# Order and engines of the post-norm chains, the gate rows and the final norm in a two-block transformer kernel

## The chip, the cores and the metric

The kernel runs on one core of a Trainium2 chip. The metric is the device time of one execution in microseconds (us). All times below were taken on the chip; the profile is that of one execution.

## The reference, cut to what matters

Two transformer blocks are computed for one sequence of 256 tokens of width 2048, all in f32. In the first block the vector c gives six rows of modulation; g_a and g_f are the gates.

```python
mod = c_act @ ada_w + ada_b
sh_a, sc_a, g_a, sh_f, sc_f, g_f = jnp.split(mod, 6, axis=-1)
h = modulate(rms_norm(x, attn_pre_norm), sh_a, sc_a)
y = hybrid_mixer(h, ...)                     # latent and differential attention, ends in @ w_o
x = x + g_a[:, None, :] * rms_norm(y, attn_post_norm)
h = modulate(rms_norm(x, ffn_pre_norm), sh_f, sc_f)
y = conv_geglu_ffn(h, w_up, conv_w, conv_b, w_down)
x = x + g_f[:, None, :] * rms_norm(y, ffn_post_norm)
# second block
h = rmsnorm(x, norm_g); proj = h @ w_in_2    # sparse and windowed attention
x = x + concat([y_a, y_b]) @ w_out_2
out = rmsnorm(x, final_g)
```

## The kernel before, in words

**Weights.** All weights come as one stream of pieces of 512 KB, [128 x 1024] f32, which SP's queue loads into twelve buffers (`raw`, line 270). Most pieces are split into a high part, rounded to the one-pass type fp32r (`hi`, a cast on ScalarE, line 292), and the rest (`lo`, a subtraction on VectorE, line 293). A product is then three one-pass matmuls: x_hi with hi, x_hi with lo, x_lo with hi. Only the modulation takes raw f32 weights: on TensorE in products of 32 rows (line 472), or on VectorE (lines 514 to 516).

**Order.** The program is a list of units of weights. Between units, small pieces of other work written as generators (softmax, gates, statistics) are advanced by a turn each; a `yield` leaves the rest to a later turn. Each engine has one queue, executed in order; a scheduler sets what stands in it from these turns and the dependences.

**Places that the change touches.** `job_y` multiplies the two token halves t = 0, 1 (128 rows each) by four groups of 512 columns, n (g in the code) = 0 to 3, one k tile after the other; it computes w_o, w_down and w_out. At its last k tile the sums go to `y_stats`, which adds the earlier part (line 1208), multiplies by the gate row (line 1213) and takes three sums of squares and products (lines 1212, 1215, 1216). In `p_ffn` the first YK of the 44 k tiles of w_down are done amid the work on w_up and the others at the end.

When all groups are in, `post` reduces the sums over the groups and computes two reciprocal roots for the two token halves: ry, that of y's post-norm, and r1, that of the new x's pre-norm, which is formed from the sums without the new x itself. Each root is a scaling (line 606), a square root on ScalarE (line 607) and four steps on VectorE (lines 608 to 611). Then `make_h` goes through eight pairs of k tiles: `x_new` updates x (line 1247) and scales it by r1 (line 1249), `x_turn` transposes it on TensorE (line 700) and writes the modulated high and low parts for the products (lines 1272 to 1274, or 1266 and 1267 in block 2). The next stage's first product is line 331. There are two such junctions: out of w_o into the FFN, and out of w_down into block 2.

The gates are made ahead of that. `gate_start` loads four rows `gw` and a bias `brow`. For the attention, `ada_rows` adds `brow` to the modulation's sum in PSUM (line 563) and spreads each of four rows over all partitions by a product with a constant (line 567). For the FFN, `ada_fold` does the same for one group at a time (lines 577 and 580). At the end `fin` computes the last root for both halves and scales and stores eight tiles (lines 1497 to 1500).

Of the kernel before, what the change touches and what calls it, by code (L numbers as in the profile page):

```python
# [13 lines left out]
F32 = mybir.dt.float32  # L14
F32R = mybir.dt.float32r
# [120 lines left out]
class Body:  # L136
# [295 lines left out]
    def job_y(self, mat, groups, kts, x, evac):  # L432
        out = []
        kts = list(kts)
        box = {}
        for n, kt in enumerate(kts):
            for g in groups:
                def fn(wt, o, n=n, kt=kt, g=g):
                    mm = self.nc.tensor.matmul
                    hi, lo = wt  # L440
                    f, l = n == 0, n == len(kts) - 1
                    if f and o == 0:
                        box[g] = [self.ps() for _ in range(2)]
                    c = slice(o * 128, o * 128 + hi.shape[-1])
                    xk = x(kt)
                    for t in range(2):
# [111 lines left out]

    def ada_rows(self, ps):
        nc = self.nc  # L560
        self.gate_start(0)
        sb = self.w()
        nc.vector.tensor_tensor(out=sb, in0=self.brow, in1=ps, op=ALU.add)
        yield
        for n in range(4):
            ps2 = self.ps()
            nc.tensor.matmul(ps2, self.cst("jsel", n, n + 1).to_broadcast([P, P]), sb, start=True, stop=True)
            yield
            nc.vector.tensor_tensor(out=self.gw[n], in0=self.gw[n], in1=ps2, op=ALU.mult)
            self.gdone[n] = True  # L570

    def ada_fold(self, acc, n):
        nc = self.nc
        a = slice(32 * n, 32 * n + 1)
        if n == 0:
            self.gate_start(1)
        nc.vector.tensor_tensor(out=acc[a], in0=acc[a], in1=self.brow[a], op=ALU.add)
        yield
        ps = self.ps()
        nc.tensor.matmul(ps, self.cst("ones"), acc, start=True, stop=True)  # L580
        yield
        nc.vector.tensor_tensor(out=self.gw[n], in0=self.gw[n], in1=ps, op=ALU.mult)
        self.gdone[n] = True


    def split(self, dst, src):
# [140 lines left out]
    def setup(self):  # L727
# [21 lines left out]
        nc.scalar.dma_start(self.ct, self.io["cst"])  # L749
        nc.scalar.dma_start(self.vt, self.io["vecs"])  # L750
        self.mod = cp.tile([P, 96], F32, tag="mod", name="mod")
        self.dtab = cp.tile([P, 3, 8, 4], BF16, tag="dtab", name="dtab")
        cb = self.cb = cp.tile([P, 5, P], BF16, tag="cb", name="cb")
        self.identb, self.mcau, self.mband = cb[:, 0], cb[:, 1:3], cb[:, 3:5]
# [81 lines left out]
    def small(self):  # L836
        nc = self.nc
        V, S = nc.vector, nc.scalar
        l4 = self.vec("lam")
        pr, ls, le = self.s(64), self.s(2), self.s(2)  # L840
        for j in range(2):
# [376 lines left out]

    def rowsum(self, a):
        o = self.s(2)  # L1220
        self.nc.vector.tensor_reduce(out=o, in_=a.rearrange("p (t n) -> p t n", t=2), axis=AX.X, op=ALU.add)
        return o

    def post(self):
        V = self.nc.vector
        sy, sxz, szz = self.rowsum(self.sy), self.rowsum(self.sxz), self.rowsum(self.szz)
        ry = self.ry = self.rsqrt_fast(sy, 2, 1.0 / D)
        t = self.s(2)
        V.tensor_tensor(out=t, in0=szz, in1=ry, op=ALU.mult)
        V.tensor_tensor(out=t, in0=sxz, in1=t, op=ALU.add)  # L1230
        V.tensor_tensor(out=t, in0=t, in1=ry, op=ALU.mult)
        V.tensor_tensor(out=self.sxx, in0=self.sxx, in1=t, op=ALU.add)
        self.r1 = self.rsqrt_fast(self.sxx, 2, 1.0 / D)
        self.gw = self.brow = None
        self.hs = {}
        self.xr = {}

    def x_new(self, i):
        V = self.nc.vector
        n, o = i // 2, (i % 2) * T  # L1240
        xr = self.xr[i] = self.w()
        with self.tc.issue_after(self.rs.ins):
            for t in range(2):
                x, z = self.xn[n, t], self.accy[n, t]
                if i < 2 or o == 0:
# [3 lines left out]
                V.tensor_scalar(out=xr[:, t * T:t * T + T], in0=x[:, o:o + T], scalar1=self.r1[:, t:t + 1], scalar2=None,  # L1249
                                op0=ALU.mult)  # L1250

    def x_turn(self, i, al, sh):
        nc = self.nc
        V, S = nc.vector, nc.scalar
        xr = self.xr.pop(i)
        ps = self.ps()
        for j in range(2):
            for t in range(2):
                self.transpose(ps[:, j * T + t * 128:j * T + t * 128 + 128], xr[:, t * T + j * 128:t * T + j * 128 + 128])
        for j in range(2):  # L1260
            k = 2 * i + j
            src = ps[:, j * T:j * T + T]
            a = al[:, k:k + 1]
            h = self.hs[k] = self.g(F32R)
            if sh is None:
                S.activation(h[:, :T], src, AF.Identity, bias=0.0, scale=a)
                V.scalar_tensor_tensor(out=h[:, T:], in0=src, scalar=a, in1=h[:, :T].bitcast(F32),
                                       op0=ALU.mult, op1=ALU.subtract)
            else:
                b = sh[:, k:k + 1]  # L1270
                f = xr[:, j * T:j * T + T]
                S.activation(h[:, :T], src, AF.Identity, bias=b, scale=a)  # L1272
                S.activation(f, src, AF.Identity, bias=b, scale=a)
                V.tensor_sub(h[:, T:], f, h[:, :T].bitcast(F32))

    def make_h(self, kt, al, sh):
        if kt == 0:
# [69 lines left out]
    def p_block2(self):  # L1347
# [123 lines left out]
        def mid2():  # L1471
            self.fg = [self.g() for _ in range(4)]
            for n in range(4):
                nc.sync.dma_start(self.fg[n], self.io["rows"][8 + n])
            self.sy = self.s(8)
            self.load_sqrt()

        def ev2(n, t, ps):
            x = self.xn[n, t]
            c = slice(4 * t + n, 4 * t + n + 1)  # L1480
            V.tensor_add(x, x, ps)
            sq = self.w()
            S.activation(sq, x, AF.Square, accum_out=self.sy[:, c])
            o = self.xn[n, t] = self.g()
# [5 lines left out]

        def fin():
            self.drain()
            r = self.rsqrt_fast(self.rowsum(self.sy), 2, 1.0 / D)
            for i, (n, t) in enumerate(sorted(self.xn)):
                a = self.xn[n, t]
                if i % 3 == 2:
                    S.activation(a, a, AF.Identity, scale=r[:, t:t + 1], bias=0.0)
                else:
                    V.tensor_scalar(out=a, in0=a, scalar1=r[:, t:t + 1], scalar2=None, op0=ALU.mult)
                nc.sync.dma_start(self.io["out"][4 * t + n], a)  # L1500
        return prog + self.call(fin)

    def compress(self, src, mat, pcol):
# [326 lines left out]
```

## Time and profile before

| | |
|---|---|
| Times of three runs, us | 1708.7, 1703.77, 1709.03 (median 1708.7) |
| Profiled execution, us | 1710.42 |
| its span, first to last instruction, us | 1708.5 |
| mean granted TensorE clock | 0.983 |
| PE busy | 1652.9 us, 97% |
| VectorE (DVE) busy | 1222.6 us, 72% |
| ScalarE (ACT) busy | 929.8 us, 54% |
| GpSimd (POOL) busy | 9.1 us, 1% |
| read from memory | 378.83 MB, 223 GB/s over the span |

Times inside the span count from its start. Shares of busy time are means over stages. PE is TensorE, PEld its weight load, SP the engine that issues most loads and stores. In a row of the timeline, the number in brackets is the engine's idle time ahead of the instruction, with what ended it. A granted clock of 1.00 is TensorE's full speed of 2.4 GHz, 0.50 the lower one of 1.2 GHz. In names of matmuls, `ps<-hi,g` is a product of tiles hi and g summed into PSUM.

### The profile page before, as it was taken

How to read it: one execution, taken by the hardware profiler on the slowest of the kernel's cores; microseconds unless marked ns; L12 is line 12 of the kernel's file. 1: busy time of each engine (PE TensorE's matmuls, PEld its weight loads, DVE VectorE, ACT ScalarE, POOL GpSimd, SP SyncE). 2: the span in 40 equal slices, each digit the busy share in tenths (PEclk: the TensorE clock that was granted, in tenths of full speed). 3: DMA queues.
4: the chain of work that ended last, by engine and by line, in shares of the span. 5: the costliest groups of instructions: out<-in, count | busy, mean ns of one | idle time of the engine just before them, and what ended most of it. 6: DMA issues, size and time to landing. Idle time of an engine off the chain costs nothing.

```text
span 1708.5 us, 27826 instructions
## 1 busy us (share of the span) xinstructions
PE 1652.9 (97%) x9968; PEld 1363.4 (80%) x9968; DVE 1222.6 (72%) x2499; ACT 929.8 (54%) x1949; POOL 9.1 (1%) x25
## 2 busy tenths in 40 slices
PE   6999999899979999999999999999979999999997
PEld 3778877667559888888888888888869888888885
DVE  6766678676776987888556777776676767777765
ACT  3444448545446766666444566665544445555643
POOL 0000000000000000000000000000000000000000
PEclk8999999999989999999999999999989999999998
DMA  9878975787965667666666665555645773344451
GB/s 381 319 280 301 335 271 186 265 348 305 387 249 169 218 222 252 223 226 217 237 221 242 220 203 186 189 187 191 195 143 176 249 255 131 124 140 140 144 185 50
DMA packets 108138, 382.74 MB, mean 224 GB/s; under 512 B 12128, under 2 KB 12384, under 8 KB 108000
## 3 DMA queue, kind: packets, MB, share of 16 engines
q1 hardware_dynamic: 107136, 379.28, 63.7%
q8 instruction: 78, 1.28, 0.3%
q10 hardware_dynamic: 864, 1.69, 0.3%
q14 instruction: 60, 0.49, 0.1%
HBM read 378.83 MB, written 2.10 MB: 223 GB/s over the span
## 4 chain that ended last, share of the span: by engine, by line
PE 93%; DVE 3%; DMA 2%; ACT 1%; issue 0%; ACTq 0%; SPq 0%; DVEq 0%
PE ps L339 24%; PE ps L340 12%; PE ps L449 8%; PE ps L450 8%; PE ps L451 8%; PE ps L331 6%; PE ps L332 5%; PE ps L333 5%; PE ps L472 4%; PE ps L700 2%; PE ps L423 2%; PE ps L424 1%; PE ps L425 1%; DVE lo L293 1%; PE ps L1690 1%; PE ps L1006 1%
## 5 line engine op out<-in xcount | busy, mean ns | idle before, releaser
L292 ACT CAST hi<-raw 128x512 fp32r<-128x512 f32 x989 | 610.0, 622 | 588.9 <-PE ps L339 194.0
L293 DVE TENSOR_TENSOR lo<-raw,hi 128x512 fp32r<-128x512 f32 x989 | 672.7, 689 | 308.9 <-ACT hi L292 303.7
L339 PE MATMUL ps<-g,hi 128*128 128x512 f32 x1744 | 621.9, 401 | 0.0
L340 PE MATMUL ps<-g,lo 128*128 128x256 f32 x1744 | 489.8, 281 | 0.0
L339 PEld LDWEIGHTS ps<-g,hi 128*128 128x128 f32 x1744 | 327.6, 188 | 82.8 <-issue 2.4
L340 PEld LDWEIGHTS ps<-g,lo 128*128 128x128 f32 x1744 | 329.6, 189 | 0.8 <-issue 0.7
L449 PE MATMUL ps<-hi,g 128*128 128x512 f32 x608 | 240.9, 398 | 1.5 <-ACT hi L292 1.5
L450 PE MATMUL ps<-lo,g 128*128 128x512 f32 x608 | 237.1, 390 | 0.6 <-DVE lo L293 0.6
L451 PE MATMUL ps<-hi,g 128*128 128x512 f32 x608 | 237.1, 390 | 0.0
L331 PE MATMUL ps<-g,hi 128*128 128x256 f32 x752 | 220.9, 296 | 1.2 <-ACT g L1272 0.7
L332 PE MATMUL ps<-g,hi 128*128 128x256 f32 x752 | 214.0, 285 | 0.0
L333 PE MATMUL ps<-g,lo 128*128 128x256 f32 x752 | 213.7, 285 | 0.0
L331 PEld LDWEIGHTS ps<-g,hi 128*128 128x128 f32 x752 | 144.9, 194 | 24.5 <-ACT hi L292 12.4
L332 PEld LDWEIGHTS ps<-g,hi 128*128 128x128 f32 x752 | 145.5, 194 | 2.4 <-issue 1.4
L333 PEld LDWEIGHTS ps<-g,lo 128*128 128x128 f32 x752 | 145.3, 193 | 0.8 <-issue 0.8
L449 PEld LDWEIGHTS ps<-hi,g 128*128 128x128 f32 x608 | 113.7, 188 | 39.5 <-issue 7.8
L450 PEld LDWEIGHTS ps<-lo,g 128*128 128x128 f32 x608 | 114.2, 188 | 25.9 <-DVE lo L293 2.7
L451 PEld LDWEIGHTS ps<-hi,g 128*128 128x128 f32 x608 | 114.1, 188 | 24.1
L516 DVE SCALAR_TENSOR_TENSOR w<-raw,csil,w 128x512 f32<-128x512 f32 x105 | 78.7, 749 | 21.1 <-DMA raw<-wstream 20.2
L472 PE MATMUL ps<-raw,cz 128*32 128x512 f32 (+1 forms) x608 | 83.0, 582 | 0.0
L938 DVE TENSOR_TENSOR g<-g,ps 128x512 f32<-128x512 f32 (+1 forms) x48 | 31.8, 664 | 44.0 <-PE ps L333 43.9
L700 PE MATMUL ps<-ct,w 128*128 128x128 f32 x248 | 37.8, 279 | 18.8 <-DVE w L1249 18.8
(273 smaller groups left out, 1510.5 us busy)
## 6 DMA issues: line engine op xcount, KB each, us to landing
raw<-wstream SPq DMA_DIRECT2D x704, 512.0 KB, 4.3
g<-rows SPq DMA_DIRECT2D x12, 256.0 KB, 4.5
g<-xt SPq DMA_DIRECT2D x8, 256.0 KB, 5.5
g<-xn SPq DMA_DIRECT2D x8, 256.0 KB, 5.4
out<-g SPq DMA_DIRECT2D x8, 256.0 KB, 2.8
g<-brow SPq DMA_DIRECT2D x2, 256.0 KB, 5.8
g<-ropes ACTq DMA_DIRECT2D x2, 256.0 KB, 3.6
vt<-vecs ACTq DMA_DIRECT2D x1, 459.5 KB, 4.2
```

Source lines behind the costliest of these rows:

```text
L292: self.nc.scalar.copy(hi[:, :n], src)
L293: self.nc.vector.tensor_sub(lo[:, :n], src, hi[:, :n].bitcast(F32))
L331: i = mm(o, hi, x[:, :T], start=first, stop=False)
L332: mm(o, hi, x[:, T:], start=False, stop=False)
L333: mm(o, lo, x[:, :T], start=False, stop=last)
L339: mm(ps, hi, x, start=first, stop=False)
L340: mm(ps[:, T:], lo, x[:, :T], start=False, stop=last)
L449: mm(ps[:, c], xh, hi, start=f and o == 0, stop=False)
L450: mm(ps[:, c], xh, lo, start=False, stop=False)
L451: mm(ps[:, c], xl, hi, start=False, stop=l and c.stop == 512)
L472: mm(box["ps"][32 * q:32 * q + 32, o * 128:e], self.cz[:, a:a + 32], wt, start=first, stop=last and kt >= 12 and e == n * 128, tile_positi ...
L516: V.scalar_tensor_tensor(out=a, in0=w, scalar=c, in1=a, op0=ALU.mult, op1=ALU.add)
```

## The change

Seven edits, in the diff below: YK goes from 26 to 24. In `job_y`, at group 3, the second half's products of the last k tile but one are held back until the first half's of the last one have been issued. The gate rows are copied out of PSUM on ScalarE, the bias is added six turns later (for the FFN six turns before the first group's add), and each row is spread by two one-pass products of a high and a low part (`gate_rows`). The load of the table for the square root moves from the start of the stage to group 2's first sum. `root` runs the reciprocal on VectorE beside the square root on ScalarE, and `post` arranges its formula around that. The first pair's x is updated in `post` by GpSimd (first half) and by ScalarE and GpSimd (second half); later pairs' updates are ordered after the low part of the pair before. `fin` does the halves one after the other. `selr` holds the constants of the gate products in fp32r.

```diff
-YK = 26
+YK = 24
...
+                    one(0)
+                    if g == 3 and n == len(kts) - 2:
+                        held.append(lambda: one(1))
+                        return
+                    while held:
+                        held.pop(0)()
+                    one(1)
...
     def ada_rows(self, ps):
         nc = self.nc
+        sb = self.w()
+        nc.scalar.copy(sb, ps)
         self.gate_start(0)
-        sb = self.w()
-        nc.vector.tensor_tensor(out=sb, in0=self.brow, in1=ps, op=ALU.add)
-        yield
-        for n in range(4):
-            ps2 = self.ps()
-            nc.tensor.matmul(ps2, self.cst("jsel", n, n + 1).to_broadcast([P, P]), sb, start=True, stop=True)
+        for _ in range(6):
             yield
-            nc.vector.tensor_tensor(out=self.gw[n], in0=self.gw[n], in1=ps2, op=ALU.mult)
-            self.gdone[n] = True
+        nc.vector.tensor_add(sb, sb, self.brow)
+        yield from self.gate_rows(sb, lambda n: self.selr[:, n:n + 1].to_broadcast([P, P]), range(4))
...
+    def gate_rows(self, sb, sel, ns):
+        nc = self.nc
+        hi, lo = self.w(F32R), self.w(F32R)
+        nc.scalar.copy(hi, sb)
+        nc.vector.tensor_sub(lo, sb, hi.bitcast(F32))
+        yield
+        for n in ns:
+            ps = self.ps()
+            nc.tensor.matmul(ps, sel(n), hi, start=True, stop=False)
+            nc.tensor.matmul(ps, sel(n), lo, start=False, stop=True)
+            yield
+            nc.vector.tensor_tensor(out=self.gw[n], in0=self.gw[n], in1=ps, op=ALU.mult)
+            self.gdone[n] = True
...
     def y_second(self, mat, kts, x, groups):
         def start():
             self.sy, self.szz, self.sxz = self.s(8), self.s(8), self.s(8)
-            self.load_sqrt()
...
         V.tensor_add(y, y, ps)
+        if c.start == 2:
+            self.load_sqrt()
...
+    def root(self, m):
...
+        self.nc.scalar.activation(q, m, AF.Sqrt)
+        V.reciprocal(iv, m)
+        V.tensor_tensor(out=u, in0=q, in1=iv, op=ALU.mult)
+        V.scalar_tensor_tensor(out=v, in0=u, scalar=-0.5, in1=q, op0=ALU.mult, op1=ALU.mult)
+        self.rs = V.scalar_tensor_tensor(out=v, in0=v, scalar=1.5, in1=u, op0=ALU.add, op1=ALU.mult)
+        return v, iv
...
+        V.tensor_scalar(out=m, in0=sy, scalar1=1.0 / D, scalar2=EPS, op0=ALU.mult, op1=ALU.add)
+        self.ry, iv = self.root(m)
+        V.tensor_tensor(out=a1, in0=szz, in1=iv, op=ALU.mult)
+        V.tensor_tensor(out=a2, in0=a1, in1=self.sxx, op=ALU.add)
+        V.tensor_scalar(out=a3, in0=a2, scalar1=1.0 / D, scalar2=EPS, op0=ALU.mult, op1=ALU.add)
+        V.tensor_tensor(out=t, in0=sxz, in1=self.ry, op=ALU.mult)
+        V.scalar_tensor_tensor(out=m1, in0=t, scalar=1.0 / D, in1=a3, op0=ALU.mult, op1=ALU.add)
+        G, zs = self.nc.gpsimd, self.w()
+        x = [self.xn[0, u][:, :T] for u in range(2)]
+        o = [zs[:, u * T:u * T + T] for u in range(2)]
+        G.tensor_scalar(out=o[0], in0=self.accy[0, 0][:, :T], scalar1=self.ry[:, 0:1], scalar2=None, op0=ALU.mult)
+        G.tensor_tensor(out=x[0], in0=x[0], in1=o[0], op=ALU.add)
+        self.r1, _ = self.root(m1)
+        self.nc.scalar.activation(o[1], self.accy[0, 1][:, :T], AF.Identity, scale=self.ry[:, 1:2], bias=0.0)
+        G.tensor_tensor(out=x[1], in0=x[1], in1=o[1], op=ALU.add)
...
-        with self.tc.issue_after(self.rs.ins):
+        with self.tc.issue_after(self.rs.ins if i == 0 else self.ht[i - 1].ins):
...
-        ps = self.ps()
+        ps = [self.ps(), self.ps()] if i == 0 else [self.ps()] * 2
...
+            for t in range(2):
+                q, m = self.s(1), self.s(1)
+                V.tensor_reduce(out=q, in_=self.sy[:, 4 * t:4 * t + 4], axis=AX.X, op=ALU.add)
+                V.tensor_scalar(out=m, in0=q, scalar1=1.0 / D, scalar2=EPS, op0=ALU.mult, op1=ALU.add)
+                r, _ = self.root(m)
+                for n in range(4):
+                    a = self.xn[n, t]
+                    if n % 2 == t:
+                        S.activation(a, a, AF.Identity, scale=r, bias=0.0)
+                    else:
+                        V.tensor_scalar(out=a, in0=a, scalar1=r, scalar2=None, op0=ALU.mult)
+                    nc.sync.dma_start(self.io["out"][4 * t + n], a)
```

Lines of the changed kernel that the orders below name: 480 is the modulation's product (472 before), 595 and 596 the two gate products, 716 the transpose (700), 450 to 452 the triple of `job_y` (449 to 451), 1249 to 1252 the root's steps, 1259 to 1274 `post`, 1289 and 1291 the update and scaling of x (1247 and 1249), 1317 the low part (1274).

PE's queue at the attention's gate, before; `ct` is the constant, `w_4294` the row sum with its bias:

```order
2480 L423 MATMUL ps_4301<-hi_4157,g_3092 128x512
2481 L424 MATMUL ps_4301<-lo_4158,g_3092 128x512
2482 L425 MATMUL ps_4301<-hi_4157,g_3092 128x512
2483 L567 MATMUL ps_4308<-w_4294,ct 128x512
2484 L567 MATMUL ps_4327<-w_4294,ct 128x512
2485 L472 MATMUL ps_4333<-raw_4033,cz 32x512
2486 L472 MATMUL ps_4333<-raw_4037,cz 32x512 x2
2487 L472 MATMUL ps_4333<-raw_4040,cz 32x512
2488 L567 MATMUL ps_4345<-w_4294,ct 128x512
2489 L423 MATMUL ps_4351<-hi_4214,g_3087 128x512
2490 L424 MATMUL ps_4351<-lo_4215,g_3087 128x512
```

The same place after; `w_4402` and `w_4403` are the high and the low part of the row sum:

```order
2503 L480 MATMUL ps_4331<-raw_4215,cz 32x512 x2
2504 L480 MATMUL ps_4331<-raw_4267,cz 32x512
2505 L716 MATMUL ps_4396<-ct,w_3544 128x128
2506 L595 MATMUL ps_4414<-w_4402,selr 128x512
2507 L716 MATMUL ps_4396<-ct,w_3544 128x128 x3
2508 L595 MATMUL ps_4434<-w_4402,selr 128x512
2509 L450 MATMUL ps_4441<-hi_4299,g_3817 128x512
2510 L451 MATMUL ps_4441<-lo_4300,g_3817 128x512
2511 L596 MATMUL ps_4414<-w_4403,selr 128x512
2512 L596 MATMUL ps_4434<-w_4403,selr 128x512
```

The gate's first product stood directly behind the triples of lines 423 to 425. Now four more such triples and sixteen modulation products stand between (rows 2483 to 2504, of which the last two listed lines are shown), and transposes and other products lie between the gate's high and low ones.

VectorE's queue at the junction into the FFN, before, from the second root's reciprocal on:

```order
709 L608 RECIPROCAL t_5749<-t_5750 128x2
710 L609 SCALAR_TENSOR_TENSOR t_5750<-t_5749 128x2
711 L610 TENSOR_TENSOR t_5750<-t_5750,t_5748 128x2
712 L611 SCALAR_TENSOR_TENSOR t_5749<-t_5750,t_5749 128x2
713 L1247 SCALAR_TENSOR_TENSOR g_5174<-g_5435,t_5735,g_5174 128x256
714 L1247 SCALAR_TENSOR_TENSOR g_5176<-g_5443,t_5735,g_5176 128x256
715 L1249 TENSOR_SCALAR w_5757<-g_5174,t_5749 128x256
716 L1249 TENSOR_SCALAR w_5757<-g_5176,t_5749 128x256
717 L1247 SCALAR_TENSOR_TENSOR g_5174<-g_5435,t_5735,g_5174 128x256
718 L1247 SCALAR_TENSOR_TENSOR g_5176<-g_5443,t_5735,g_5176 128x256
719 L1247 SCALAR_TENSOR_TENSOR g_5178<-g_5460,t_5735,g_5178 128x512
720 L1247 SCALAR_TENSOR_TENSOR g_5180<-g_5468,t_5735,g_5180 128x512
```

The same place after:

```order
710 L1249 RECIPROCAL t_5771<-t_5751 128x2
711 L1250 TENSOR_TENSOR t_5772<-t_5770,t_5771 128x2
712 L1251 SCALAR_TENSOR_TENSOR t_5773<-t_5772,t_5770 128x2
713 L1252 SCALAR_TENSOR_TENSOR t_5773<-t_5773,t_5772 128x2
714 L1291 TENSOR_SCALAR w_5782<-g_5186,t_5773 128x256
715 L1291 TENSOR_SCALAR w_5782<-g_5188,t_5773 128x256
716 L1317 TENSOR_TENSOR g_5791<-w_5782,g_5791 128x256
717 L1317 TENSOR_TENSOR g_5795<-w_5782,g_5795 128x256
718 L1289 SCALAR_TENSOR_TENSOR g_5186<-g_5445,t_5756,g_5186 128x256
719 L1289 SCALAR_TENSOR_TENSOR g_5188<-g_5453,t_5756,g_5188 128x256
720 L1291 TENSOR_SCALAR w_5799<-g_5186,t_5773 128x256
```

And GpSimd's rows around that junction after (the row ahead and the row behind belong to other places):

```order
13 L1002 MEMSET g_2929 128x512
14 L1269 TENSOR_SCALAR w_5767<-g_5445,t_5756 128x256
15 L1270 TENSOR_TENSOR g_5186<-g_5186,w_5767 128x256
16 L1273 TENSOR_TENSOR g_5188<-g_5188,w_5767 128x256
17 L1269 TENSOR_SCALAR w_13677<-g_12933,t_13666 128x256
```

The two updates of line 1247 ahead of the scalings of line 1249 (now 1291) are gone; their work stands on GpSimd and ScalarE. The reciprocal reads the value under the root, `t_5751`, and no longer the root itself. The four updates that followed the scalings directly now come behind the first pair's low parts (line 1317), pair by pair.

## Rows read from the trace of the kernel before

**Rows 1.** The page: busy time by engine (part 1), a costly group (part 5).

```profile
PE 1652.9 (97%) x9968; PEld 1363.4 (80%) x9968; DVE 1222.6 (72%) x2499; ACT 929.8 (54%) x1949; POOL 9.1 (1%) x25
...
L293 DVE TENSOR_TENSOR lo<-raw,hi 128x512 fp32r<-128x512 f32 x989 | 672.7, 689 | 308.9 <-ACT hi L292 303.7
```

**Rows 2.** Waits of PE: who waited for whom, us, times, longest.

```profile
PE ps L700 <- DVE w L1249: 18.8, 2, 9.9
```

**Rows 3.** Chain of waits around the attention's gate: start, us, what.

```profile
331.20 7.17 DMA g<-brow
...
339.23 3.75 PE ps L567 x4
342.98 1.78 PE ps L472 x8
```

**Rows 4.** Timeline of PE there: start, us, operation, count, idle before it.

```profile
323.13 1.07 PE L472 MATMUL ps<-raw,cz 128*32 128x512 f32 x8
...
339.23 3.75 PE L567 MATMUL ps<-w,ct 128*128 128x512 f32 x4 [6.34 <-DVE t L594]
```

**Rows 5.** Windows: busy us by engine, granted clock, DMA share, GB/s.

```profile
336.00:352.00 16.00, 12.77 (x52) 5.30 (x56) 7.64 (x24) 2.98 (x6) 0.00 (x0) 0.79 0.46 160
352.00:384.00 32.00, 32.00 (x162) 24.45 (x151) 27.32 (x58) 14.64 (x38) 0.00 (x0) 1.00 1.02 406
```

**Rows 6.** Chain: a fold's gate product; a one-pass product of 512 columns.

```profile
783.99 0.86 PE ps L580 x2
...
1693.95 0.23 PE ps L451
```

**Rows 7.** Timeline at the junction into the FFN.

```profile
492.73 0.39 PE L451 MATMUL ps<-hi,g 128*128 128x512 f32 x1
493.06 1.28 DVE L1208 TENSOR_TENSOR g<-g,ps 128x512 f32<-128x512 f32 x2
...
497.68 0.16 DVE L606 TENSOR_SCALAR t<-t 128x2 f32<-128x2 f32 x1
...
501.99 1.16 PE L700 MATMUL ps<-ct,w 128*128 128x128 f32 x4 [8.87 <-DVE w L1249]
...
503.81 1.01 PE L331 MATMUL ps<-g,hi 128*128 128x256 f32 x3 [0.66 <-ACT g L1272]
```

**Rows 8.** Timeline at the junction into block 2.

```profile
1249.99 0.39 PE L451 MATMUL ps<-hi,g 128*128 128x512 f32 x1
...
1254.81 1.01 POOL L1514 MEMSET g<- 128x512 f32 x2 [49.66 <-DVE w L1216]
1254.85 1.28 ACT L607 ACT_TABLE_LOAD   x1
1254.94 0.41 DVE L606 TENSOR_SCALAR t<-t 128x2 f32<-128x2 f32 x1
...
1261.99 1.22 PE L331 MATMUL ps<-g,hi 128*128 128x256 f32 x4 [0.56 <-ACT g L1266]
```

**Rows 9.** GpSimd's groups by form: names, shapes, count, busy us, mean ns.

```profile
L1514 POOL MEMSET g<- 128x512 f32 x4 | 2.1, 531 | 71.3 <-DVE w L1216 49.7 <-DVE g L1247 13.4 <-PE ps L700 8.2
...
L747 POOL TENSOR_TENSOR cz<-s,s 128x16 f32<-128x16 f32 x1 | 0.2, 228 | 0.1
```

**Rows 10.** DVE's groups by form, then line 1274 in the FFN's first pass.

```profile
L1249 DVE TENSOR_SCALAR w<-g,t 128x256 f32<-128x256 f32 x32 | 10.4, 348 | 0.0
...
L1247 DVE SCALAR_TENSOR_TENSOR g<-g,t,g 128x512 f32<-128x512 f32 x12 | 8.8, 746 | 0.0
...
L1274 DVE TENSOR_TENSOR g<-w,g x16: 416/426/428, 504.2 to 548.5; 128x256 fp32r<-128x256 f32 x16
```

**Rows 11.** The end: timeline, and a window of the stores.

```profile
1696.51 0.39 PE L451 MATMUL ps<-hi,g 128*128 128x512 f32 x1
...
1700.67 4.48 SPq L1500 DMA_DIRECT2D out<-g  x8
...
1702.00:1706.00 4.00, 0.00 (x0) 0.00 (x0) 0.62 (x2) 0.00 (x0) 0.00 (x0) 0.50 1.01 383
```

More of the change, by code (lines that the diff above doesn't have):

```diff
@@ L445, in fn, with one @@
                     xk = x(kt)
-                    for t in range(2):
+                    def one(t):
                         xh, xl = xk[:, t * 128:t * 128 + 128], xk[:, T + t * 128:T + t * 128 + 128]
@@ L576, in ada_fold @@
             self.gate_start(1)
+            for _ in range(6):
+                yield
         nc.vector.tensor_tensor(out=acc[a], in0=acc[a], in1=self.brow[a], op=ALU.add)
-        yield
-        ps = self.ps()
[L580 to L583, printed above, removed]
+        yield from self.gate_rows(acc, lambda n: self.selr[:, 4:5].to_broadcast([P, P]), [n])
+    def gate_rows(self, sb, sel, ns):
[3 more added lines that the diff above has]
+        nc.vector.tensor_sub(lo, sb, hi.bitcast(F32))
+        yield
+        for n in ns:
[5 more added lines that the diff above has]
+            self.gdone[n] = True
     def split(self, dst, src):
@@ L751, in setup @@
         self.mod = cp.tile([P, 96], F32, tag="mod", name="mod")
+        self.selr = cp.tile([P, 5], F32R, tag="selr", name="selr")
         self.dtab = cp.tile([P, 3, 8, 4], BF16, tag="dtab", name="dtab")
@@ L838, in small @@
         V, S = nc.vector, nc.scalar
+        S.copy(self.selr[:, 0:4], self.cst("jsel", 0, 4))
+        S.copy(self.selr[:, 4:5], self.cst("ones", 0, 1))
         l4 = self.vec("lam")
@@ L1222, in rowsum @@
         return o
+    def root(self, m):
+        V = self.nc.vector
+        n = m.shape[-1]
+        q, iv, u, v = self.s(n), self.s(n), self.s(n), self.s(n)
+        self.nc.scalar.activation(q, m, AF.Sqrt)
[4 more added lines that the diff above has]
+        return v, iv
     def post(self):
@@ L1226, in post @@
         sy, sxz, szz = self.rowsum(self.sy), self.rowsum(self.sxz), self.rowsum(self.szz)
[L1227 to L1233, printed above, removed]
+        m, a1, a2, a3, t, m1 = [self.s(2) for _ in range(6)]
+        V.tensor_scalar(out=m, in0=sy, scalar1=1.0 / D, scalar2=EPS, op0=ALU.mult, op1=ALU.add)
[13 more added lines that the diff above has]
+        G.tensor_tensor(out=x[1], in0=x[1], in1=o[1], op=ALU.add)
+        V.tensor_tensor(out=self.sxx, in0=a2, in1=t, op=ALU.add)
         self.gw = self.brow = None
@@ L1236, in post @@
         self.xr = {}
+        self.ht = {}
     def x_new(self, i):
@@ L1241, in x_new @@
         xr = self.xr[i] = self.w()
-        with self.tc.issue_after(self.rs.ins):
+        with self.tc.issue_after(self.rs.ins if i == 0 else self.ht[i - 1].ins):
             for t in range(2):
                 x, z = self.xn[n, t], self.accy[n, t]
-                if i < 2 or o == 0:
+                if i == 1 or i and o == 0:
                     a = slice(o, o + T) if i < 2 else slice(0, 512)
@@ L1248, in x_new @@
                                            op0=ALU.mult, op1=ALU.add)
-                V.tensor_scalar(out=xr[:, t * T:t * T + T], in0=x[:, o:o + T], scalar1=self.r1[:, t:t + 1], scalar2=None,
-                                op0=ALU.mult)
+                V.tensor_scalar(out=xr[:, t * T:t * T + T], in0=x[:, o:o + T], scalar1=self.r1[:, t:t + 1],
+                                scalar2=None, op0=ALU.mult)
     def x_turn(self, i, al, sh):
@@ L1255, in x_turn @@
         xr = self.xr.pop(i)
-        ps = self.ps()
+        ps = [self.ps(), self.ps()] if i == 0 else [self.ps()] * 2
         for j in range(2):
             for t in range(2):
-                self.transpose(ps[:, j * T + t * 128:j * T + t * 128 + 128], xr[:, t * T + j * 128:t * T + j * 128 + 128])
+                self.transpose(ps[j][:, j * T + t * 128:j * T + t * 128 + 128],
+                               xr[:, t * T + j * 128:t * T + j * 128 + 128])
         for j in range(2):
             k = 2 * i + j
-            src = ps[:, j * T:j * T + T]
+            src = ps[j][:, j * T:j * T + T]
             a = al[:, k:k + 1]
@@ L1266, in x_turn @@
                 S.activation(h[:, :T], src, AF.Identity, bias=0.0, scale=a)
-                V.scalar_tensor_tensor(out=h[:, T:], in0=src, scalar=a, in1=h[:, :T].bitcast(F32),
-                                       op0=ALU.mult, op1=ALU.subtract)
+                self.ht[i] = V.scalar_tensor_tensor(out=h[:, T:], in0=src, scalar=a, in1=h[:, :T].bitcast(F32),
+                                                    op0=ALU.mult, op1=ALU.subtract)
             else:
@@ L1481, in ev2 @@
             V.tensor_add(x, x, ps)
+            if c.start == 2:
+                self.load_sqrt()
             sq = self.w()
```

12 lines of the change are left out of this document (2 added, 10 removed).

## Prediction, made before the changed kernel was run

> **What bounds the kernel now.** I read the page first, then PE's waits, then the chain of waits around each long one, then the windows. The page has PE busy for 97% of the span [rows 1]: whatever makes the kernel shorter must take work off PE or close a hole in it. Two kinds of hole are left in mid-program. PE's waits name line 700, the first transpose behind each post-norm, twice, 18.8 us together [rows 2]; the timeline has one more, 6.34 us before line 567, the first gate product of the attention [rows 4]. The end of the span, after the last product, is a third place. All three are what the diff edits, so I price it place by place, and last the products themselves. The sum is made against the profiled execution, 1710.42 us (span 1708.5); the median of the runs is 1708.7, so 1.7 is taken off at the end. About 0.3%, here 5 us, is what a measurement of this kernel can tell from no change.
>
> **Gate of the attention, at 332 us.** The chain stands on the load of brow: issued at 331.20, landed 7.17 us later, then line 563's add, then line 567 [rows 3]. PE, with no other work ahead of line 567 in its queue, idles 6.34 us [rows 4]. The granted clock over the next 16 us is 0.79 [rows 5], which shows in the work itself: the first two products take 3.75 instead of 2 x 0.86 (a fold product at full clock [rows 6]), and eight matmuls of line 472 take 1.78 where the same eight took 1.07 before the hole [rows 3, 4]. Hole and clock together: 6.34 + 2.03 + 0.71 = 9.08.
> After the change six turns of other work lie between the loads and the add. By the order PE has ahead of its first gate product, from the work that stood behind it, 16 matmuls of the modulation (four of the order's are the eight records of 1.07 [rows 4], so about 4 us) and four triples of one-pass products (12 x 0.23 = 2.8 [rows 6]). Their weights stand early in the load order, and I take them as there. PE then reaches the gate at 332.9 (339.23 - 6.34) + 6.7 = 339.6. brow is there at 338.4; add 0.69, cast about 0.65, put the high half at 339.8 and the low half, behind four small scalings on DVE, near 341. I take 0.7 of new wait (0 if brow comes earlier, 2 if its load is pushed back by pieces that now start sooner).
> What is late next is the weight stream. In those 16 us the DMA engines were busy 0.46 of the time, 8.6 us unused, because all buffers were full and only PE frees them; from 352 to 384 they run at 1.02, 406 GB/s, while PE is always busy [rows 5]. PE comes early by up to 9.1 + 1.6 (below) and the stream by 8.6 at most, so up to 2.1 (10.7 - 8.6) could be given back as waits for weights; PE did not wait there before, so some stock exists. I take 0.8. Place: 9.08 - 0.7 - 0.8 = 7.6, ends 5 and 9.1.
>
> **Gate products, eight.** One f32 product costs PE 0.86; two one-pass products of 512 columns cost 2 x 0.23 [rows 6]. 8 x 0.40 = 3.2. Each pays a cast on ACT and a subtraction on DVE; both engines wait for PE there, and PE is elsewhere occupied, so nothing on the path. Ends 2.5 and 3.7 (the first fold could lose its own short wait too).
>
> **Post-norm into the FFN, at 493 us.** PE's last product ends at 493.12 (492.73 + 0.39); DVE, still on a subtraction, starts on the two sums at 493.06 and is gapless until the scaling at 497.68; the first transpose starts at 501.99, the first FFN product at 503.81, 10.69 behind PE's end [rows 7]. (a) With the first half's products put ahead, its sum can start when PE has two triples left, 6 x 0.23 = 1.38 before the end instead of at the end; but two weight subtractions of 0.69 [rows 1] now stand inside the stretch instead of one, and the second half still waits for the last product. Counted step by step, the scaling comes 0.43 earlier: 4.13 behind PE's end for 4.56. (b) The chain from it to r1 is 16 steps of about 0.2 now; with reciprocal beside root, and a1, a2, a3 beside the first root's tail, it has 12 or so: 3.2 becomes 2.4. (c) Behind r1 DVE has two x updates and two scalings; now two scalings alone, if GpSimd is done in time. No row has GpSimd at 256 columns of arithmetic. Two-input work of 16 columns takes 0.228 and a fill of 512 takes 0.531 [rows 9], so a fill's rate gives about 0.43 for 256 columns, and twice that rate about 0.65. I take 0.45 and 0.7, near the upper: scaling and two additions 1.85 behind the first root, where r1 needs 1.3. The second half's scaling waits some 0.6. (d) With two PSUM tiles ACT starts behind two transposes, not four: half of 1.16. Together 4.13 + 2.4 + 0.6 + 0.35 (a scaling [rows 10]) + 0.58 + 0.66 (ACT, as now: 1.82 - 1.16) = 8.72, with hand-overs 8.75 behind PE's end: 1.9 gained, ends 0.3 (GpSimd at three times my figure) and 2.6 (hidden altogether).
> The Trainium skill (GPSIMD Engine Reference, section 3.1) gives 2.6 cycles per element at 1.2 GHz for a two-input operation, which is by estimate 0.55 us for 256 columns plus dispatch. No run so far shows that operation at this size; by it the sum would stay within 0.1 us.
>
> **Post-norm into block 2, at 1250 us.** Same chain, with one row more: ACT loads a table at 1254.85 for 1.28 us, to 1256.13, ahead of a root whose input comes from the scaling at 1254.94 and which would start a step of 0.2 later: it is late by 1.0; the first product stands at 1261.99, 11.61 behind PE's end at 1250.38 [rows 8]. The load moves to group 0's sums, several microseconds earlier, where ACT waits for PE; no Gelu is left behind it that would switch back. 11.61 - 8.7 = 2.9 gained, ends 1.2 and 3.6.
> The Trainium skill (ScalarE: Activation LUTs, What ACT_TABLE_LOAD costs) puts a switch at 1.28 plus 1.38 of draining. The row here has the root right behind the 1.28, so the trace does not agree that the second part is paid; were it paid, the gain would be 1.38 larger.
>
> **The end.** The last product ends at 1696.90, the first store is issued at 1700.67 and stores run at 1.01 of the DMA engines, 383 GB/s [rows 11]: from there the end is bandwidth. The first half's sum now starts a triple or two earlier and its root does not wait for the second half: first store 0.7 to 0.8 earlier, the second half's stores queued in time behind it. 0.75, ends 0 (a store of the second half late, since ACT's second root stands behind two scalings in its queue) and 1.3.
>
> **At nothing:** the split point of w_down (24 for 26; the matmuls and pieces are the same in number, only when they are done moves; -1 to +1), and the table load ahead of the FFN (ACT idles there).
>
> Sum: 7.6 + 3.2 + 1.9 + 2.9 + 0.75 = 16.35; 1710.4 - 16.35 = 1694.1 against the profiled execution, 1692.4 against the median. I predict 1693.
>
> **Rivals.**
> A. The hole at the gate is only moved. For it: PE's queue is in order, brow's load still takes 7 us behind weight pieces, and the stream is full from 352 on. Against it: PE's new rows fill 6.7 us. If all but 1 of the 7.6 went, 1700.
> B. GpSimd holds DVE up. For it: the one scaling of two columns that ran beside a fill on GpSimd took 0.41 instead of 0.16 [rows 7, 8]. The second root's four DVE steps and the sxx addition run beside GpSimd: 5 x 0.25 = 1.25, and additions twice as long delay the second half by 1.2 more: 2.4 per junction, 4.9 in all, 1698. The Trainium skill (GPSIMD Engine Reference, section 1) has GpSimd share its SBUF interface with DVE's instructions of two SBUF inputs, as these are; a rule against the change, and the one row bears it out only for an instruction of another kind.
> C. Slower, by the x pairs. Each later pair's update is now ordered after the low half of the pair before, no longer right after the root. The low halves come about every 6.2 us per pair (16 in eight pairs from 504.2 to 548.5), and behind one lie up to two updates of 0.746 and two scalings of 0.348 [rows 10], 2.2, then transposes and ACT, 1.2: about 3.4 of 6.2, before the weight subtractions between them. If DVE's queue puts four of those (4 x 0.69) in the way, 6.2, and each pair comes just in time. For the kernel to be slower, the 14 steps of both junctions must each make PE wait over 1.5 us (16.35 + 5 over 14): 1714. Against it: DVE's load per pair leaves room, and by the order at most two stand between.
> D. Nothing of note: A and B together with a stall or two of C, about 1706; the change then does its work at places where PE finds other waits.
>
> **How the numbers follow.** Forecast 0.70 (1693, own range 1688 to 1698); A 0.12; B 0.08; D 0.06; C 0.04. The forecast, A and B are over 5 us below the median, 0.90, of which I take 0.02 off for A with more lost: faster 0.88; within 0.3% D and that, 0.08; slower C, 0.04. Low end: all terms at their good ends are 9.1 + 3.7 + 2.6 + 3.6 + 1.3 = 20.3, 1688, less 1 for the split point. High end: A with B's half, 1702.
>
> **What would show it.** After: no wait of PE over 1 us at its first gate product and a granted clock of 1.0 in the 16 us behind it; gate products of about 0.46; transposes behind each post-norm 6.5 to 7.5 us after PE's end; no table load between the last sum and the first root; POOL rows of 0.4 to 0.8 us beside DVE steps of 0.16 to 0.2; first store near 3.0 us behind PE's end. PE waiting for brow's add or for weights at 340 to 400 us would make A right, DVE steps stretched beside POOL B, and new waits of PE for line 1291 or 1315 at many pairs C.

## The result, and the profile after

The changed kernel takes 1693.04 us (median of four runs, 1692.54 to 1693.11), the one before 1708.87 in the same comparison: a ratio of 0.9911, 95% interval 0.9889 to 0.9933. The forecast was 1693, from 16.35 us of gain; 15.8 were measured, and 17.6 between the two profiled spans (1708.5 and 1690.9). That the total came out is partly luck: one term had the wrong sign, another was too small.

The spans can be cut at the same places in both traces. "To the first transposes" ends at the first transpose row after 255 us; E1, E2 and E3 are the ends of the last products ahead of the two post-norms and of the program's end.

| Stretch | before | after | gained | forecast |
|---|---|---|---|---|
| start to the first transposes | 262.95 | 260.24 | 2.7 | 0 |
| from there to E1 (gate of the attention) | 230.17 | 219.28 | 10.9 | 7.6 + 1.6 |
| E1 to the FFN's first product | 10.69 | 9.11 | 1.6 | 1.9 |
| from there to E2 (four gate products) | 746.57 | 744.63 | 1.9 | 1.6 |
| E2 to block 2's first product | 11.61 | 11.80 | -0.2 | 2.9 |
| from there to E3 | 434.91 | 435.09 | -0.2 | 0 |
| E3 to the end of the span | 11.60 | 10.75 | 0.85 | 0.75 |

PE's waits after, the lines that answer to [rows 2] and [rows 4]:

```profile
PE ps L716 <- DVE w L1291: 18.2, 2, 10.5
...
PE ps L716 <- ACT w L590: 0.7, 1, 0.7
...
PE ps L495 <- DVE w L524: 0.6, 1, 0.6
```

The 6.34 ahead of the gate is gone, 0.7 stands in its place (booked on line 716, whose transpose stands directly ahead of the gate's first product). But the two waits for the first transposes are still 18.2 together, and the longest of them has grown from 9.9 to 10.5.

**The gate.** The chain after, at the place of [rows 3]:

```profile
328.84 7.22 DMA g<-brow
...
336.08 0.70 DVE w L574
...
336.81 0.63 ACT w L590
...
337.51 0.30 PE ps L716
...
340.47 0.23 PE ps L595
340.69 0.23 PE ps L596
```

and the windows of [rows 5]:

```profile
336.00:352.00 16.00, 15.33 (x77) 11.26 (x70) 15.41 (x34) 6.55 (x16) 0.00 (x0) 1.00 1.03 408
352.00:384.00 32.00, 32.00 (x161) 25.17 (x159) 23.84 (x54) 16.34 (x44) 0.00 (x0) 1.00 0.87 324
```

Bias and cast are still on the chain, but PE comes to them only 0.67 early. A gate row costs 0.23 + 0.23 where it cost 0.86 [rows 6]. The clock stays at 1.00 (0.79 before), and the DMA engines, half idle in these 16 us before, run at 1.03; the stretch behind needs them less.

**The first junction.** Timeline after, beside [rows 7]:

```profile
479.13 0.39 PE L452 MATMUL ps<-hi,g 128*128 128x512 f32 x1
...
483.40 0.15 DVE L1259 TENSOR_SCALAR t<-t 128x2 f32<-128x2 f32 x1
...
484.61 0.94 POOL L1269 TENSOR_SCALAR w<-g,t 128x256 f32<-128x256 f32 x1 [381.67 <-DVE t L1262]
...
485.63 0.72 POOL L1270 TENSOR_TENSOR g<-g,w 128x256 f32<-128x256 f32 x1
485.80 0.57 DVE L1252 SCALAR_TENSOR_TENSOR t<-t,t 128x2 f32<-128x2 f32 x1
486.32 0.72 POOL L1273 TENSOR_TENSOR g<-g,w 128x256 f32<-128x256 f32 x1
486.48 0.97 DVE L1291 TENSOR_SCALAR w<-g,t 128x256 f32<-128x256 f32 x2
...
487.24 1.16 PE L716 MATMUL ps<-ct,w 128*128 128x128 f32 x4 [7.73 <-DVE w L1291]
...
488.63 1.22 PE L331 MATMUL ps<-g,hi 128*128 128x256 f32 x4 [0.23 <-ACT g L1315]
```

The scaling comes 3.88 behind PE's end (479.52), earlier than forecast (4.13). Then VectorE's step of line 1252, 0.16 elsewhere, takes 0.57 and ends when GpSimd's first addition ends, and the two scalings of line 1291, 0.61 together in x_dve below, take 0.97 beside its second one.

**The second junction.** Timeline after, beside [rows 8]:

```profile
1232.87 0.39 PE L452 MATMUL ps<-hi,g 128*128 128x512 f32 x1
...
1237.14 0.16 DVE L1259 TENSOR_SCALAR t<-t 128x2 f32<-128x2 f32 x1
...
1240.22 3.75 DVE L1291 TENSOR_SCALAR w<-g,t 128x256 f32<-128x256 f32 x2
1240.72 1.91 POOL L1410 MEMSET g<- 128x512 f32 x4
1242.58 0.99 POOL L1562 MEMSET g<- 128x512 f32 x2
...
1243.77 1.16 PE L716 MATMUL ps<-ct,w 128*128 128x128 f32 x4 [10.51 <-DVE w L1291]
...
1245.06 1.01 PE L331 MATMUL ps<-g,hi 128*128 128x256 f32 x3
```

No table load stands here any more, and the scaling is ready 3.88 behind PE's end (1233.26). All of that is lost in two scalings of 0.35 each that take 3.75; the line's own rows in this stretch (minimum, median, maximum in ns) say which:

```profile
L1291 DVE TENSOR_SCALAR w<-g,t x2: 333/1912/3491, 1240.2 to 1243.6; 128x256 f32<-128x256 f32 x2
```

One took 3.49: it began beside GpSimd's second addition and ended at 1243.71, just behind the last of six fills of 128 x 512 on GpSimd (1243.57). Before, four of these fills (line 1367 there) ran between 1181 and 1205, in GpSimd's idle time; the last three, from GpSimd's own rows:

```profile
1203.36 0.53 POOL L1367 MEMSET g<- 128x512 f32 x1 [20.89 <-DVE g L1213]
1204.16 0.99 POOL L1367 MEMSET g<- 128x512 f32 x2 [0.28 <-PE ps L451]
```

GpSimd's queue is in order: the change put three operations ahead of them that wait for ry, so the fills were pushed to just behind these, next to the scaling that PE waits for.

**The end.** The first store is issued 2.91 behind the last product (3.77 before, [rows 11]):

```profile
1679.76 0.39 PE L452 MATMUL ps<-hi,g 128*128 128x512 f32 x1
...
1683.06 4.49 SPq L1548 DMA_DIRECT2D out<-g  x8
```

### The profile page after: what moved, and what is told of

Same layout as the page of the kernel before. It is cut to its first block, busy times and chain, and to the rows that moved or that the text cites. A ratio compares the mean times of both kernels' runs of the same rounds, so it can differ in the third digit from the quotient of the medians.

```text
span 1690.9 us, 27851 instructions
## 1 busy us (share of the span) xinstructions
PE 1643.1 (97%) x9968; PEld 1361.7 (81%) x9968; DVE 1224.4 (72%) x2506; ACT 932.7 (55%) x1962; POOL 13.5 (1%) x31
## 4 chain that ended last, share of the span: by engine, by line
PE 93%; DVE 4%; DMA 2%; ACT 1%; issue 0%; ACTq 0%; DVEq 0%
PE ps L339 24%; PE ps L340 12%; PE ps L450 8%; PE ps L452 7%; PE ps L451 7%; PE ps L331 6%; PE ps L332 5%; PE ps L333 5%; PE ps L480 4%; PE ps L716 2%; PE ps L423 2%; PE ps L424 1%; PE ps L425 1%; DVE lo L293 1%; DMA raw<-wstream 1%; PE ps L1738 1%
## 5 line engine op out<-in xcount | busy, mean ns | idle before, releaser
L716 PE MATMUL ps<-ct,w 128*128 128x128 f32 x248 | 37.9, 279 | 18.9 <-DVE w L1291 18.2
```

## Experiments

Single profiles differ by chance in two places, read below: the start, and how long the clock stays low behind a junction. So the stretches from E1 and E2 to the next first product are compared first; in kernels that differ elsewhere they agree within 0.05 us (9.11 three times for the first).

**mem_away: the fills away from the second junction.**

```diff
+            self.pre = [self.g() for _ in range(4)]
+            for u in self.pre:
+                nc.gpsimd.memset(u, 0.0)
             self.post()
...
-            for t in E["vbz"] + E["kbz"]:
-                nc.gpsimd.memset(t, 0.0)
...
-                nc.gpsimd.memset(t, 0.0)
+                V.memset(t, 0.0)
```

> The changed kernel with its six fills around the second junction taken off GpSimd's queue behind the pair's update: four are issued ahead of the post-norm chain, two run on VectorE later. Theory: at the junction into block 2 the first scaling on VectorE (3.49 us instead of 0.34) was held by these fills, which the change had pushed behind GpSimd's three new operations. Then the time from PE's last product to the first product of block 2 falls from 11.80 to about 9.1, as at the other junction, and the kernel to about 1690.3. Rival 1: GpSimd's arithmetic itself, or the low clock, makes that junction slow: 11.8 stays, 1693. Rival 2: the fills only wait elsewhere: gain under 1.

Measured: 1689.95 (1689.66 to 1691.46), ratio 0.9894 (0.9877 to 0.991). E2 to the first product: 9.03. Its timeline:

```profile
1233.27 0.39 PE L452 MATMUL ps<-hi,g 128*128 128x512 f32 x1
...
1240.63 0.97 DVE L1291 TENSOR_SCALAR w<-g,t 128x256 f32<-128x256 f32 x2
...
1241.39 1.17 PE L716 MATMUL ps<-ct,w 128*128 128x128 f32 x4 [7.73 <-DVE w L1291]
...
1242.69 1.01 PE L331 MATMUL ps<-g,hi 128*128 128x256 f32 x3
```

Same rows but for the fills, and 3.75 becomes 0.97. Both rivals fall.

**fill_first: six fills put at the first junction, where none were.**

```diff
+        last = G.tensor_tensor(out=x[1], in0=x[1], in1=o[1], op=ALU.add)
+        if not getattr(self, "filled", False):
+            self.filled = True
+            with self.tc.issue_after(last.ins):
+                for _ in range(6):
+                    G.memset(self.w(), 0.0)
```

> The changed kernel with six fills of 128 x 512 more on GpSimd, directly behind its three operations at the first junction, as they stand by accident at the second. Theory: back-to-back fills hold VectorE's scaling: it takes about 3.5 us instead of 0.71, the first product of the FFN comes 11.8 behind PE's end instead of 9.1, and the kernel is 2.7 slower, about 1695.7. Rival: the second junction's long scaling has another cause (the loads that ScalarE issues there, the clock): the first stays at 9.1 and the time at 1693.

Measured: one run, 1696.4. E1 to the first product: 11.90.

```profile
480.71 0.39 PE L452 MATMUL ps<-hi,g 128*128 128x512 f32 x1
...
488.06 3.75 DVE L1296 TENSOR_SCALAR w<-g,t 128x256 f32<-128x256 f32 x2
488.56 2.85 POOL L1278 MEMSET w<- 128x512 f32 x6
...
491.61 1.16 PE L716 MATMUL ps<-ct,w 128*128 128x128 f32 x4 [10.52 <-DVE w L1296]
...
493.00 1.22 PE L331 MATMUL ps<-g,hi 128*128 128x256 f32 x4 [0.23 <-ACT g L1320]
```

The same 3.75 now at a junction with no loads on ScalarE's queue. That the fills hold the scaling is shown from both sides.

**x_dve: the first pair's update back on VectorE.**

```diff
-        G.tensor_scalar(out=o[0], ...)
-        G.tensor_tensor(out=x[0], in0=x[0], in1=o[0], op=ALU.add)
...
-        self.nc.scalar.activation(o[1], ...)
-        G.tensor_tensor(out=x[1], in0=x[1], in1=o[1], op=ALU.add)
...
-                if i == 1 or i and o == 0:
+                if i < 2 or o == 0:
```

> The changed kernel with the first pair's update back on VectorE (as in the kernel before), GpSimd and ScalarE not used for it; all else as changed. Theory: GpSimd's operations stretch VectorE's steps beside them (0.33 and 0.57 for 0.16) and take 0.94 + 0.72 + 0.72, so they bring nothing: from PE's end to the first product about 8.85 at the first junction (9.11 now), and about 8.8 at the second (11.80), since the fills run early again; kernel about 1689.8. Rival, by which the move was worth its price: the two updates add their 0.87 to the chain, 9.6 and 9.6, kernel about 1691.3.

Measured: 1690.26 (1689.58 to 1691.54), ratio 0.9894 (0.988 to 0.9909); 8.79 and 8.83 at the junctions. The first one:

```profile
480.77 0.39 PE L452 MATMUL ps<-hi,g 128*128 128x512 f32 x1
...
485.04 0.16 DVE L1259 TENSOR_SCALAR t<-t 128x2 f32<-128x2 f32 x1
...
487.28 0.16 DVE L1252 SCALAR_TENSOR_TENSOR t<-t,t 128x2 f32<-128x2 f32 x1
487.36 0.87 DVE L1282 SCALAR_TENSOR_TENSOR g<-g,t,g 128x256 f32<-128x256 f32 x2
488.15 0.61 DVE L1284 TENSOR_SCALAR w<-g,t 128x256 f32<-128x256 f32 x2
...
488.56 1.17 PE L716 MATMUL ps<-ct,w 128*128 128x128 f32 x4 [7.39 <-DVE w L1284]
```

From the scaling to r1 it takes 2.4 (487.44 - 485.04), the figure of the forecast; with GpSimd beside it, it took 2.97 (486.37 - 483.40). From there to the transposes it takes 1.12 (488.56 - 487.44), and in the changed kernel, where GpSimd's second addition stretches the scalings, 0.87 (487.24 - 486.37). So the two updates, 0.87 of VectorE's time, cost the chain 0.25, and GpSimd's company cost it 0.57. The rival (9.6) falls: moving the pair off VectorE cost 0.3 at the first junction and 3.0 at the second.

**only_gate: the kernel before with the new gate rows and YK 24 alone.** Its edit is the new `ada_rows`, `ada_fold`, `gate_rows` and `selr` of the diff above.

> The kernel before with the new gate rows (late add of the bias, two one-pass products) and YK 24, nothing else. Theory: the hole at the attention's gate, its low clock and eight products are worth 10.4 + 1.6 = 12: 1696.9. Rival: a part of the 10.4 came from other parts of the change or from the start of the program, where the changed kernel's profile is 2.7 ahead by 262 us: only 9, 1699.7.

Measured: 1696.25 (1695.76 to 1698.26), ratio 0.9931 (0.9916 to 0.9945): 12.2 of the 15.8 come from this edit. From the first transposes to E1 it takes 220.29 us, so 9.9 of the stretch's gain.

**gate_f32: the late add, but one f32 product.**

```diff
-            nc.tensor.matmul(ps, sel(n), hi, start=True, stop=False)
-            nc.tensor.matmul(ps, sel(n), lo, start=False, stop=True)
+            nc.tensor.matmul(ps, sel(n), sb, start=True, stop=True)
```

> The changed kernel with the late add of the bias, but one f32 product for each gate row. Theory: hole and product are separate: no idle over 1 us ahead of the gate, products of 0.86 instead of 0.46, so 8 x 0.4 = 3.2 slower, about 1696.2. Rival: without the cast on ScalarE the wait ahead of the gate (0.67) goes, and the one-pass products bring only about 2.5.

Measured: one run, 1693.64, only 0.6 slower. The products cost 0.86 again and the wait ahead of the gate is 0.6, so hole and product are separate, as the theory has it. The wait is now for the scaling on VectorE that the transpose reads (line 1071), so the rival's 0.67 did not go with the cast. The stretch to E1 is 2.2 longer, the FFN's is equal (744.65). There the four products do take 0.40 more each, but from the first of them to the second the chain needs 102.96 (665.58 to 768.54) where the changed kernel needs 104.90 (662.78 to 767.68) for the same 592 matmuls; why they ran closer together no run shows. Another part of the 3.2 is hidden by chance: block 2's stretch is 1.1 shorter, the clock having risen 2.7 us behind the first product and not 5.3. What the product is worth in the kernel's time isn't settled by one run; by the rows it is 0.40 for each.

**yk24: the kernel before with YK 24 alone** (`-YK = 26`, `+YK = 24`).

> The kernel before with the split of w_down at 24 instead of 26, nothing else. Theory: no difference, 1708.5 within 1.5. It also shows the start of the program without the new constants: if the clock at 22 us rises as late as in the profile of before (64 modulation records in 6.14 us), the start's 2.7 us belong to something in the change; if it takes 4.7 to 5.5 as in the five later profiles, they were chance. Rival: the split moves work out of the end and is worth 1 us or more.

Measured: 1708.74 (1706.88 to 1712.18, ten runs), ratio 1.0 (0.9988 to 1.0012): the split is worth nothing. The first transposes, in yk24 and then in fill_first, which has all of the change:

```profile
260.09 0.60 PE L700 MATMUL ps<-ct,w 128*128 128x128 f32 x4
```

```profile
262.62 0.60 PE L716 MATMUL ps<-ct,w 128*128 128x128 f32 x4
```

Here they come early without the change and late with it. In the twelve profiles they lie between 259.9 and 262.95, so the start's 2.7 us between the two profiles are chance, not the change.

**x_dve_oldload: x_dve with the table load back at the start of the stage.**

```diff
+            self.load_sqrt()
...
-        if c.start == 2:
-            self.load_sqrt()
```

> x_dve with the load of the root's table back at the start of the stage. Theory: at the second junction the table is then loaded directly ahead of the first root (1.28 us), and the first product comes 1.0 later than in x_dve, 9.8 for 8.8; the first junction and the rest stay: about 1691.2. Rival: the load is hidden there by the shorter chain, no difference.

Measured: one run, 1692.27; 8.79 and 9.12. The second junction:

```profile
1239.35 1.28 ACT L1247 ACT_TABLE_LOAD   x1
...
1239.99 0.29 DVE L1258 TENSOR_SCALAR t<-t 128x2 f32<-128x2 f32 x1
...
1240.64 0.20 ACT L1247 ACTIVATE t<-t 128x2 f32<-128x2 f32 x1
...
1245.24 1.01 PE L331 MATMUL ps<-g,hi 128*128 128x256 f32 x3
```

The load is there again, but it costs 0.3, not 1.0: it starts 0.64 ahead of the scaling that feeds the root (0.09 in [rows 8]), since VectorE now has one more weight subtraction in the stretch, and so runs mostly beside it.

**x_dve_nohold: x_dve with the old order of the last two k tiles** (`if g == 3 and n == len(kts) - 2` made `if False`).

> x_dve without the held second half: the last two k tiles in the old order. Theory: the first half's sum starts 0.69 or more later, the scaling ahead of the first root 0.43 later, so the first products come 9.2 behind PE's end for 8.8 and the end is 0.4 to 0.7 longer (11.2 for 10.7): in all about 1.3 slower, 1691.6. Rival: VectorE's queue is the bound whatever the order, no difference at the junctions.

Measured: one run, 1693.02; 9.46 and 9.63 at the junctions, 11.36 at the end (8.79, 8.83 and 10.72 with the hold): 0.67, 0.80 and 0.64, 2.1 in all, more than expected. The first junction:

```profile
481.44 0.39 PE L452 MATMUL ps<-hi,g 128*128 128x512 f32 x1
...
491.29 1.01 PE L331 MATMUL ps<-g,hi 128*128 128x256 f32 x3 [0.23 <-ACT g L1308]
```

**late_lo and late_conv: what stands next in the chain.** In late_lo the weight subtractions of the next stage go behind the first pair's scalings, in late_conv their casts go behind the second root as well.

```diff
+            def sub(hi=hi, lo=lo, src=src, n=n, p=a // PB):
+                self.nc.vector.tensor_sub(lo[:, :n], src, hi[:, :n].bitcast(F32))
+                self.used(p)
...
+        self.x_new(0)
+        with self.tc.issue_after(self.tail.ins):
+            while self.owed:
+                self.owed.pop(0)()
```

> The changed kernel with the first pair's update on VectorE (as in x_dve) and, at both junctions, the weight subtractions for the next stage that stood inside the post-norm chain put behind the first pair's scalings. Theory: VectorE is the path from PE's last product to the second root, so two subtractions of 0.6 us less shorten each junction by 1.2: first product 7.6 behind PE's end instead of 8.8, kernel about 1687.7. Rival: the next stage's first products then wait for these low parts (up to four of 0.69 after the scalings), and 1 us or more of it comes back as new waits of PE behind the junction: about 1690.

> late_lo with the casts of these weights on ScalarE put behind the second root as well (in late_lo the post-norm's sums on VectorE waited 0.44 for ScalarE's squares, among which two casts of 0.6 stood). Theory: with ScalarE's queue free too, the first product comes 7.9 behind PE's end at both junctions (8.4 in late_lo, 8.8 in x_dve), and the kernel takes about 1688.5. Rival: the casts now come late for the next stage, its first products wait for them, and the time stays at 1689.5 or rises.

Measured: late_lo 1689.46 (1688.31 to 1691.27), ratio 0.9879 (0.9862 to 0.9897), junctions 8.43 and 8.40; late_conv 1690.44 (1689.38 to 1691.32), 0.9901 (0.9885 to 0.9918), junctions 7.96 and 7.93. In late_lo only 0.4 of the 1.2 came: with its own queue shorter, VectorE waits for ScalarE's squares. late_conv removes that, its junctions are what was expected, and nothing of it reaches the time: the stretches behind them are 1.0 and 1.1 longer than in x_dve. The 7 us behind each first product (the column behind POOL is the granted clock), in x_dve and in late_conv:

```profile
489.95:496.95 7.00, 7.00 (x46) 7.00 (x47) 3.98 (x9) 4.38 (x10) 0.00 (x0) 0.76 0.04 5
1243.15:1250.15 7.00, 7.00 (x42) 7.00 (x43) 3.60 (x8) 2.15 (x4) 0.00 (x0) 0.68 0.01 5
```

```profile
487.84:494.84 7.00, 7.00 (x38) 6.92 (x39) 4.60 (x11) 3.44 (x7) 0.00 (x0) 0.61 0.42 150
1241.13:1248.13 7.00, 6.89 (x32) 6.59 (x33) 4.23 (x11) 1.62 (x3) 0.00 (x0) 0.53 0.58 195
```

0.15 less clock over 7 us is 1.05 us of work, at both places. Whether a shorter hole itself keeps the clock low for longer, or these two profiles were unlucky, stays open: over the twelve profiles the low stretch behind a first product lasted 2.8 to 6.6 us at the seven junctions under 9 us and 2.3 to 5.7 at the seventeen longer ones. With its time at the low clock counted half, the stretch from the FFN's first product to E2 takes 742.6 to 742.7 us in all nine kernels with the one-pass gate products: what moves it from one of them to the next is the clock alone.

mem_away, x_dve, late_lo and late_conv take less than both kernels: their slowest runs (1691.27 to 1691.54) lie below the changed kernel's fastest (1692.54), which was timed in another comparison. Among the four nothing is settled: late_lo has the lowest median, 0.5 to 1.0 below the others, with ranges that overlap.

## Why the prediction was right, and where not

**Gate: right, sized low.** Hole and load behaved as worked out, and the clock is back at 1.00. The new wait is 0.67 for 0.7 taken, partly by chance: in the eight other profiles with the whole new gate it is 0 to 0.5. Of the weight stream I feared 0.8; one new wait shows it, 0.6 at line 495 (0.1 to 0.85 in the others), where the modulation on VectorE waits for weights. The stretch gained 10.9 for 9.2; the eight others make it between 218.5 and 220.5, 9.6 to 11.7. One term that was too small is the clock: two rows gave 2.03 + 0.71 = 2.74, but a clock of 0.79 over 16 us [rows 5] is 0.21 x 16 = 3.4. The rest of the difference, about 1, no row assigns. Rival A, that the hole is only moved, is out.

**Gate products: right by the row,** 0.46 for 0.86.

**First junction: right, with two errors that partly cancel.** The hold was taken at 0.43 and is worth 0.67. GpSimd was taken at 0.45 and 0.7, and is 0.94 and 0.72, and it slows VectorE's steps beside it. The transposes stand 7.7 behind PE's end, and 10.5 at the second junction, outside the 6.5 to 7.5 that the prediction named as its sign. The Trainium skill (GPSIMD Engine Reference, section 3.1) gives 2.6 cycles per element for the addition, by estimate 0.55 plus dispatch; the trace's 0.72 does not contradict that, but the one-input scaling was the slower one here.

**Second junction: wrong, and this is the step that failed:** "two scalings alone, if GpSimd is done in time". It was done in time; what was queued behind it was not looked at, though in GpSimd's queue of the changed kernel the fills stand right behind the additions. That cost 2.8 (11.80 against 9.03), nearly all of the 2.9 forecast. Rival B named the mechanism, GpSimd holding VectorE up, from the one row that showed it, at 2.4 for each junction; it took 0.6 from the steps and 0.4 from the scalings at each, and 2.8 more from the fills at the second. But for GpSimd the 2.9 would nearly have come: the junction gains 2.6 in mem_away and 2.8 in x_dve. The table load, forecast at 1.0, has two prices: before, the second junction was 0.92 longer than the first, which has no load; in the new order the load costs 0.3. The prediction also misread where it goes: not to group 0's sums but to group 2's first one (`c.start == 2`). In the trace after it stands at 1155.49, 78 us ahead of PE's end, so nothing hung on that.

The Trainium skill (GPSIMD Engine Reference, section 1) says of GpSimd's SBUF interface that it contends with VectorE's instructions in a 2-port mode or with two SBUF inputs. The held steps of lines 1252 (two such inputs) and 1291 (one) bear out that there is contention; whether line 1291 runs in such a mode no run here shows. And steps of line 1250, with two inputs, kept their 0.16 beside the scaling of line 1269, and subtractions of line 293, with two inputs, their 0.69 beside fills: two inputs alone did not make VectorE wait here.

**The end: right,** 0.85 for 0.75. **The split point: right,** nothing. **Rival C (x pairs): out,** no new wait of PE at lines 1291 or 1315 but the first pair's.

So the 15.8 of the medians are 12.2 of the gate (only_gate), 1.6 and -0.2 at the junctions, 0.85 at the end, and some 1.3 that single comparisons don't resolve. 1693 was met because the second junction's missing 3.1 stood against a gate that was sized 1.4 too low (12.2 for 7.6 + 3.2) and against what isn't resolved.

## What to carry to other kernels

When work is moved onto an idle engine, read the whole queue of that engine: what ran early there, unnoticed, now runs behind the new work, at the worst moment. Before a hole is shortened by an engine that shares something with the critical one, compare it with leaving the work where it was; here VectorE alone was 0.3 and 0.2 us shorter at the junctions than with GpSimd's help and the fills out of the way (mem_away), which the kernels' times don't tell apart. The cheap gain was to give an in-order queue other work to do ahead of an instruction that waits for a load.

## What the runs showed of the hardware

- A VectorE scaling of 128 x 256 that began beside a GpSimd addition, with six fills right behind that (128 x 512, 0.52 us each), took 3.49 us, until the last fill had ended; its neighbour took its usual 0.33.
- Fills did not hold every VectorE instruction: in x_dve a subtraction of 128 x 512 (line 293, at 1237.46) took its usual 0.69 beside two fills, and the scaling of two columns behind it 0.29 for 0.16.
- Steps on VectorE of two columns took 0.57 and 0.33 for 0.16 beside GpSimd's arithmetic; in x_dve, without it, the same steps took 0.16.
- A scaling of 128 x 256 with a per-row scalar took GpSimd 0.94, an addition of the same size 0.72; VectorE does both as one operation in 0.48 [rows 10 have its 128 x 512 form].
- Behind a hole of 6.6 to 10.5 us TensorE's clock stayed at half for 2.3 to 6.6 us more of work, differently in profiles of nearly the same program, which moves a run by up to 2 us at each place.
